# A two-layer diffusion block in split fp32: element-wise sums moved off GpSimd, buffers lent to the gather handed back, one-hots built four at a time, and part of the weights multiplied whole

## The chip, the cores and the metric

The kernel runs on one core of one Trainium2 chip. The metric is the device time of one execution in microseconds (us). TensorE (PE in the profile, PEld for its weight loads) multiplies, VectorE (DVE), ScalarE (ACT) and GpSimd (POOL) do element-wise work, and SyncE (SP) issues most of the transfers.

## The reference, cut to what matters

Two streams of 256 tokens with 1024 features each, `x` and `ctx`, go through two layers. Each layer normalises, multiplies by a wide input matrix, runs three branches (differential attention, windowed attention, a gated delta-net scan), merges them, and then runs an expert layer that keeps 16 of 16,384 experts for each of 8 heads.

```
def token_mixer(h, hc, ...):
    qA, kA, vA, qB, kB, vB, qkvC, zC, aC, bC, gl = split_cols(h @ w_in)
    oA, oB, oC = diff_attention(...), window_gqa(...), gated_deltanet(...)
    return merge_branches((oA, oB, oC), gl, b_gate, w_branch, w_out)

def peer_ffn(h, wq, keys, u_tab, v_tab):
    q = (t @ wq).reshape(n, PEER_HEADS, 2, PEER_HALF)
    s = einsum('thcd,cnd->thcn', q, keys)
    sv, si = top_k(s, 16);  cand = sv[:,:,0,:,None] + sv[:,:,1,None,:]
    cv, ci = top_k(cand, 16)
    eid = (i1 * 128 + i2);  gw = softmax(cv)
    act = gelu(einsum('pd,ped->pe', tb, u_tab[eb]))
    out = einsum('pe,ped->pd', act * gb, v_tab[eb])
```

The second layer needs `ctx` only as keys, values and states; the result is `x`.

## The kernel before, in words

**Arithmetic.** Almost every large product is done in three parts. `split` (line 622 of the kernel before) makes of an fp32 tile of 128x1024 a rounded part on ScalarE (a CAST to fp32r) and a remainder on VectorE (a TENSOR_TENSOR subtract, fp32r out) or, where a caller says so, on GpSimd. `mm3` then multiplies high by high, high by low and low by high. So a loaded half of a weight chunk takes three buffers of 4 KB per partition (the pool `b4`, 36 buffers), one CAST and one subtract before TensorE can use it.

**Stages, in the order of the program.** (1) `ctx` of layer 0: norm, 28 chunks of `w_in` (256 columns each, loaded as two halves), the three branches, merge, output. (2) `route` of `ctx`: queries, top 16 by VectorE's MAX8, FIND_INDEX8 and MATCH_REPLACE8, and the decoding of the indices. (3) The same mixing for `x`. (4) The expert layer of `ctx`, done by gathering: for each of two halves of the tokens 128 indirect DMAs of rows of the first table with a dot product on VectorE (SCALAR_TENSOR_TENSOR with an accumulator), then 128 indirect DMAs of rows of the second table with a product on TensorE. GpSimd issues these DMAs. The rows live in 8 buffers, and three more tiles of the gather too, borrowed from `b4`. (5) The expert layer of `x`, done densely: `route`, then `weights`, which builds for each token a 128x128 table of its expert weights from two one-hot matrices (the stage is called build below) and writes it to HBM, then for all 128 blocks of 128 experts a product with the first table (dU, 8 steps over the features), Gelu, a multiply by the table of weights, and a product with the second table (dV). The first `PRE` blocks of dU may be done ahead of the table. (6) Layer 1: keys, values and states of `ctx`, then mixing, route, build and dense experts for `x`. There is no gather in layer 1.

**What sets the order.** The class `Rec` records all operations, and `order` (line 398) plans on the host, with a cost for every operation, in which order each engine issues them and which buffer each tile takes; the result is emitted as it stands. Operations have priorities by place in the program; `route` and `weights` have a lead of 8000 (`RBASE`). An operation that is far ahead of the oldest unfinished one (measured in `cw`, a sum of planned TensorE, VectorE and ScalarE time) is held back: beyond `FAR` it isn't started, and beyond `NEAR` it has to leave `SPARE` buffers. The gather is a lane of its own. `restore` hands borrowed buffers back: of a borrowed kind whose flag is True, when a tile of that kind is freed after the lane's last operation. Row tiles are freed before the gather's last operation, so their 8 buffers stay lent for the whole of layer 1; the planner's buffers in layer 1's dU are 28 different ones of the 36.

**Who does the subtracts and sums.** `WPOOL` gives GpSimd every second subtract of the weights of `x` in layer 0 (47 of them, with those of `route`). In layer 1, `UP1` gives it 32 of the 64 first blocks of dU, and `VP` seven of eight of the 128 blocks of dV (112). GpSimd also does the sums of rope, of merge and of the output (48 of 128x512), the scaling of matrices in the delta-net chains (144 of 128x256) and in layer 1 the sums and products in `route`.

Every instruction of these helpers is recorded at one line (603 in the profile before), so groups are told apart by tiles and shapes.

## Time and profile before

| | us |
|---|---|
| median of 3 executions | 3939.72 |
| lowest and highest of them | 3938.74, 3962.46 |
| the profiled execution | 3933.92 |
| its span (first to last instruction) | 3932.1 |
| TensorE busy in the span | 3530.0 (90%) |
| VectorE busy | 2472.8 (63%) |
| ScalarE busy | 1610.0 (41%) |
| GpSimd busy | 1481.9 (38%) |
| mean granted TensorE clock | 0.933 of full speed |

The 1.8 us between the profiled execution and its span lie outside the first and last instruction. A matmul's busy time overlaps with that of the next one, so the busy sum of a group divided by its count is what one costs in a row of them, and the mean of one is longer. The granted clock of a stretch is the mean of the two levels (1.2 and 2.4 GHz) that TensorE had in it. A whole fp32 product (not fp32r) shows as two MATMUL records, an fp32r product as one. Where the stages lie in time is known by laying each engine's order of instructions over the records: they agree one by one on VectorE, ScalarE and GpSimd.

### The profile page before, as it was taken

The page shows a single profiled execution, that of the slowest core. Times are in us where ns is not written, and L with a number is a line of the kernel's source. Part 1 is how long each engine was busy: PE and PEld are TensorE (multiplying, and loading weights), DVE is VectorE, ACT ScalarE, POOL GpSimd, SP SyncE. Part 2 cuts the span into 40 slices and gives each one's busy share as a digit, 9 for nine tenths or more (in the row PEclk, how much of TensorE's full clock was granted, in tenths as well). Part 3 has the DMA queues.
Part 4 walks back from the last instruction along what each step waited for, and adds up shares of the span by engine and source line. Part 5 has one row for each costly group of instructions (what it writes and reads, how often), then busy time and mean ns, then how long its engine had stood idle before and what let it go on. Part 6 is the DMA issues. An engine that isn't in the chain of part 4 may idle for free. (4 is left out here: it accounts for less than half of the span.)

```text
span 3932.1 us, 64402 instructions
## 1 busy us (share of the span) xinstructions
PE 3530.0 (90%) x24312; PEld 2982.5 (76%) x24312; DVE 2472.8 (63%) x5599; ACT 1610.0 (41%) x3070; POOL 1481.9 (38%) x1125
## 2 busy tenths in 40 slices
PE   7999964986997798889999999998996899899999
PEld 6787954866794467767777888877896699678998
DVE  4444579889656886897444454646559942555554
ACT  4544422433442233343333346544543343344443
POOL 1110123778364345663333202222023043675443
PEclk9999986877898999999999998988998999999999
DMA  7356742566466799999889851302351455565653
GB/s 279 112 169 239 254 168 98 184 230 233 161 206 231 252 368 376 384 409 361 334 332 333 310 195 43 103 28 89 103 197 65 129 184 170 190 222 213 221 207 142
DMA packets 300966, 837.78 MB, mean 213 GB/s; under 512 B 26736, under 2 KB 96752, under 8 KB 300656
## 3 DMA queue, kind: packets, MB, share of 16 engines
q1 hardware_dynamic: 153168, 522.80, 37.2%
q0 software_dynamic: 73728, 268.47, 18.6%
q10 hardware_dynamic: 73760, 42.40, 3.6%
q8 instruction: 192, 3.15, 0.3%
q14 instruction: 118, 0.97, 0.1%
HBM read 792.67 MB, written 40.89 MB: 212 GB/s over the span
## 5 line engine op out<-in xcount | busy, mean ns | idle before, releaser
L603 PE MATMUL ps<-b,b 128*128 128x256 f32 (+4 forms) x18528 | 2742.4, 309 | 202.7 <-DVE b L603 134.8
L603 PEld LDWEIGHTS ps<-b,b 128*128 128x128 f32 (+2 forms) x18528 | 2449.7, 192 | 476.8 <-DVE b L603 163.3
L603 DVE TENSOR_TENSOR b<-b,b 128x1024 fp32r<-128x1024 f32 (+3 forms) x1065 | 1142.8, 1106 | 817.2 <-ACT b L603 550.9
L603 ACT CAST b<-b 128x1024 fp32r<-128x1024 f32 (+1 forms) x982 | 917.4, 976 | 702.6 <-PE ps L603 297.9
L603 POOL TENSOR_TENSOR b<-b,b 128x1024 fp32r<-128x1024 f32 (+2 forms) x241 | 586.8, 2445 | 922.7 <-DVE b L603 367.5
L603 ACT COPY b<-ps 128x256 f32<-128x256 f32 (+3 forms) x896 | 291.2, 350 | 676.4 <-PE ps L603 666.6
L603 POOL DMA_INDIRECT rows<-in_u_tab,eid x256 | 357.8, 1398 | 271.1 <-DVE rows L603 118.2
L603 POOL DMA_INDIRECT rows<-in_v_tab,eidT x256 | 284.0, 1109 | 426.5 <-PE ps L603 354.6
L603 PE MATMUL ps<-b 128*128 128x128 f32 (+1 forms) x2048 | 337.9, 320 | 19.2 <-ACT b L603 7.5
L603 PE MATMUL ps<-consts,b 128*128 128x128 f32 (+1 forms) x1290 | 261.1, 316 | 103.8 <-DVE b L603 76.9
L603 ACT ACTIVATE b<-ps 128x512 f32<-128x512 f32 (+1 forms) x264 | 136.7, 520 | 523.5 <-PE ps L603 507.0
L603 PEld LDWEIGHTS ps<-b 128*128 128x128 f32 (+1 forms) x2048 | 255.7, 207 | 119.6 <-DVE b L603 39.6
L603 DVE SCALAR_TENSOR_TENSOR rows<-rows,ga 128x1024 f32<-128x1024 f32 x256 | 322.9, 1288 | 4.4 <-DMA rows<-in_u_tab,eid 2.4
L603 PEld LDWEIGHTS ps<-consts,b 128*128 128x128 f32 x1290 | 184.4, 180 | 148.2 <-issue 68.8
L603 DVE TENSOR_SCALAR b<-consts,b 128x128 f32<-128x128 f32 x1024 | 235.4, 309 | 10.8 <-DMA gd<-b 7.7
L603 PE MATMUL ps<-rows,ga 128*32 128x512 f32 x1024 | 160.5, 626 | 19.0 <-DMA rows<-in_v_tab,eidT 17.8
L603 DVE COPY_PREDICATED b<-masks,ps 128x64 f32<-128x64 uint8 (+1 forms) x416 | 83.7, 251 | 148.5 <-PE ps L603 146.9
L603 ACT COPY b<-b 128x128 f32<-128x128 f32 x384 | 108.0, 303 | 60.5 <-DVE b L603 56.1
L603 DVE TENSOR_TENSOR b<-ps,b 128x128 f32<-128x128 f32 (+4 forms) x144 | 61.9, 454 | 93.8 <-PE ps L603 57.8
L603 PEld LDWEIGHTS ps<-rows,ga 128*32 128x32 f32 x1024 | 29.5, 111 | 94.6 <-DMA rows<-in_v_tab,eidT 47.8
L603 PE MATMUL ps<-b,cs 128*32 128x256 f32 x768 | 69.8, 430 | 12.2 <-DVE cs L603 11.5
L603 ACT ACTIVATE b<-b 128x512 f32<-128x512 f32 (+1 forms) x62 | 38.9, 629 | 96.0 <-DVE b L603 42.5
(176 smaller groups left out, 1450.6 us busy)
## 6 DMA issues: line engine op xcount, KB each, us to landing
b<-in_u_cols SPq DMA_DIRECT2D x256, 512.0 KB
b<-in_v_tab SPq DMA_DIRECT2D x256, 512.0 KB
b<-in_w_in SPq DMA_DIRECT2D x184, 512.0 KB
gd<-b ACTq DMA_DIRECT2D x64, 512.0 KB
b<-gd SPq DMA_DIRECT2D x64, 512.0 KB
b<-in_w_ada SPq DMA_DIRECT2D x48, 512.0 KB
b<-in_w_ada SPq DMA_DIRECT2D x96, 256.0 KB
b<-in_wq SPq DMA_DIRECT2D x48, 512.0 KB
```

The costliest lines, as they stand in the source:

```text
L603: r = getattr(getattr(nc, o.eng), o.meth)(*[_real(x) for x in o.args], **{k: _real(x) for k, x in o.kw.items()})
```

## The change

None of the edits changes what is computed:

- GpSimd loses all subtracts (`WPOOL`, `UP1` empty, `VP = 1`), the sums of rope and of the output, and layer 1's work in `route` (`aux` stays VectorE); VectorE takes them. The scalings of the delta-net chains go to ScalarE, one per head. The sums of merge, the square roots, the rope tables and the indirect DMAs stay.
- `restore` hands back every borrowed kind once its lane is done.
- The one-hot of the second index is made for four tokens in one TENSOR_TENSOR of 128x512. Of the four weighted one-hots of the first index, one goes to ScalarE as two activations (`Abs`, then `Relu`), three stay TENSOR_SCALARs on VectorE.
- Layer 0's first 16 chunks of `w_in` for `x` (`WHOLE`) and its first 32 blocks of dU (`U4`) are multiplied in whole fp32: no CAST, no subtract, one product instead of three.
- The planner has new costs, a model of the read port that VectorE and GpSimd share, `PRE` 32 instead of 48, `FAR` 80 instead of 150, no weight in `cw` for `route` and `weights`, and a freer rule for layer 1's first part (`FREE`), once the gather is done.

```diff
-U4, V4 = (), ()
-WPOOL = (1, 3, 5, 7)
-UP0, UP1 = (), range(0, 64, 4)
+U4, V4 = range(32), ()
+WPOOL = ()
+UP0, UP1 = (), ()
-OUTV = False
+OUTV = True
-VP = 8
+VP = 1
+ACTB = (1, 1)
+TAIL, FREE1 = 0, True
+FREE = {"b4": 4, "b2": 2, "b1": 1, "ps": 0}
-PRE = 48
+PRE = 32
-NEAR, FAR = 20.0, 150.0
+NEAR, FAR, URGENT = 20.0, 80.0, 0.0
+WHOLE = range(16)
...
+        o.port = eng in ("vector", "gpsimd") and not o.dma and sum(
+            isinstance(x, V) and x.n > 1 and x.tile.kind == "sb" for x in ins) > 1
...
-        o.cw = self.cw[o.lane] = self.cw.get(o.lane, 0.0) + o.dur * LOAD.get(eng, 0.0)
+        o.lane, o.free = self.lane, self.free
+        o.cw = self.cw[o.lane] = self.cw.get(o.lane, 0.0) + o.dur * LOAD.get(eng, 0.0) * (URGENT if self.base == RBASE else 1.0)
...
-                        if dist > FAR:
+                        free = o.free and lpos[-1] >= len(lanes[-1]) - TAIL
+                        if dist > FAR and not free:
                             return "far"
...
-                if t.tag in BORROW and (not BORROW[t.tag][2] or lpos[lane] == len(lanes[lane])):
-                    restore(t.tag)
+                for tag in BORROW:
+                    if owner.get(tag) == lane and (lpos[lane] == len(lanes[lane]) or tag == t.tag and not BORROW[tag][2]):
+                        restore(tag)
...
         for k in range(n):
-            (lh, ll), (rh, rl) = lhsT(k), rhs(k)
+            a, b = lhsT(k), rhs(k)
+            if len(a) == 1 or len(b) == 1:
+                self.nc.tensor.matmul(out, a[-1], b[-1], start=(start and k == 0), stop=(stop and k == n - 1))
+                continue
+            (lh, ll), (rh, rl) = a[:2], b[:2]
...
-            w = self.g(4, [P, k // 2, n])
-            self.nc.sync.dma_start(w, src[:, h * (k // 2):(h + 1) * (k // 2)])
+            w = self.load([P, k // 2, n], src[:, h * (k // 2):(h + 1) * (k // 2)])
+            if whole:
+                out += [(w[:, j],) for j in range(k // 2)]
+                continue
...
-            nc.gpsimd.tensor_tensor(qv, qv, t1, op=OP.add)
+            nc.vector.tensor_tensor(qv, qv, t1, op=OP.add)
...
-                nc.gpsimd.tensor_tensor(m1, M1[:, None, :].to_broadcast([P, H2, P]), bc(gc), op=OP.mult)
+                for h in range(H2):
+                    nc.scalar.activation(m1[:, h], M1, AF.Copy, scale=gc[:, h:h + 1])
...
+                nc.vector.tensor_tensor(A[:, :, 0], io4, sc[:, 1, k:k + 4, None].to_broadcast([P, 4, P]), op=OP.is_equal)
                 for t in range(4):
                     k = t0 + q + t
-                    nc.vector.tensor_scalar(A[:, t, 0], self.iota, sc[:, 1, k:k + 1], None, OP.is_equal)
-                    nc.vector.tensor_scalar(A[:, t, 1], self.iota, sc[:, 0, k:k + 1], sc[:, 2, k:k + 1],
-                                            OP.is_equal, OP.mult)
+                    if t >= ACTB[l]:
+                        nc.vector.tensor_scalar(A[:, t, 1], self.iota, sc[:, 0, k:k + 1], sc[:, 2, k:k + 1],
+                                                OP.is_equal, OP.mult)
+                    else:
+                        d = A[:, t, 1]
+                        nc.scalar.activation(d, self.iota, AF.Abs, scale=-1.0, bias=sc[:, 0, k:k + 1])
+                        nc.scalar.activation(d, d, AF.Relu, scale=sc[:, 3, k:k + 1], bias=sc[:, 2, k:k + 1])
...
-                if c0 // 2 % 8 in u4:
+                if c0 in u4:
                     for k in range(KT):
-                        nc.tensor.matmul(sp[:, i], u[:, k], full[k // 4][:, k % 4], start=(k == 0), stop=(k == KT - 1))
+                        nc.tensor.matmul(sp[:, i], u[:, k], hT[k][2], start=(k == 0), stop=(k == KT - 1))
                     continue
...
+        self.whole = True
         _, (x, xs) = self.mix(0, 0, self.I["x"], pr, kv, S)
+        self.whole = False
...
-        self.aux = self.nc.gpsimd
+        pass
         self.lab("1 norm1")
+        self.nc.free = FREE1
```

Three places show what the planner makes of it.

TensorE, layer 0, the first chunk of `x` (its result is ps_6821 before, ps_6869 now; the weights are b_1417 and b_1418 before, and b_1409 and b_1410 now; a row with x4 stands for four products), before:

```order
L603 MATMUL ps_6821<-b_1418_6951,b_1470_6732 128x256
L603 MATMUL ps_6821<-b_1417_6780,b_1471_6870 128x256
L603 MATMUL ps_6821<-b_1417_6780,b_1470_6732 128x256
L603 MATMUL ps_6821<-b_1418_6951,b_1470_6732 128x256
L603 MATMUL ps_6821<-b_1417_6780,b_1471_6870 128x256
L603 MATMUL ps_6821<-b_1417_6780,b_1470_6732 128x256
```

and now, with the next chunk (ps_6938) behind it:

```order
L627 MATMUL ps_6869<-b_1409_6822,b_1467_6327 128x256 x4
L627 MATMUL ps_6869<-b_1410_6872,b_1468_6329 128x256 x4
L627 MATMUL ps_6869<-b_1409_6822,b_1467_6327 128x256 x4
L627 MATMUL ps_6869<-b_1410_6872,b_1468_6329 128x256 x4
L627 MATMUL ps_6938<-b_1409_6822,b_1475_6645 128x256 x4
```

The chunk has 48 products before (three for each of two halves of the columns and eight steps) and 16 now, and it has no VectorE subtract ahead of it.

VectorE, layer 1, the start of build (consts holds the ramp 0 to 127, the second operand the indices and weights by token), before:

```order
L603 TENSOR_SCALAR b_5787_30357<-consts_71,b_5777_30336 128x128 x4
L603 TENSOR_SCALAR b_5789_30362<-consts_71,b_5777_30336 128x128 x4
L603 TENSOR_SCALAR b_5791_30367<-consts_71,b_5777_30336 128x128 x2
L603 TENSOR_REDUCE pii_29622<-b_5774_30355 128x2x16 x2
L603 TENSOR_SCALAR b_5791_30367<-consts_71,b_5777_30336 128x128 x2
```

and now:

```order
L627 TENSOR_TENSOR b_5659_29194<-consts_71,b_5649_29190 128x4x128
L627 TENSOR_TENSOR b_5661_29196<-consts_71,b_5649_29190 128x4x128
L627 TENSOR_SCALAR b_5659_29194<-consts_71,b_5649_29190 128x128 x3
L627 TENSOR_SCALAR b_5661_29196<-consts_71,b_5649_29190 128x128 x3
L627 TENSOR_TENSOR b_5663_29198<-consts_71,b_5649_29190 128x4x128
L627 TENSOR_SCALAR b_5663_29198<-consts_71,b_5649_29190 128x128 x3
```

Eight instructions for four tokens have become four on VectorE, and two more stand on ScalarE.

VectorE, layer 1, the dense experts near the middle of dV (128x1024 are subtracts of weights, 128x2x128 the multiply by the table of weights, 128x512 the remainder of its result), before:

```order
L603 TENSOR_TENSOR b_6498_34797<-b_6496_34716,b_6497_34779 128x1024
L603 TENSOR_TENSOR b_6468_34793<-b_6468_34793,b_6469_34628 128x2x128
L603 TENSOR_TENSOR b_6468_34793<-b_6468_34793,b_6470_34646 128x2x128
L603 TENSOR_TENSOR b_6472_34840<-b_6468_34793,b_6471_34831 128x512
L603 TENSOR_TENSOR b_6501_34849<-b_6499_34718,b_6500_34821 128x1024
```

and now:

```order
L627 TENSOR_TENSOR b_6354_33342<-b_6352_33173,b_6353_33329 128x1024
L627 TENSOR_TENSOR b_6357_33354<-b_6355_33180,b_6356_33339 128x1024
L627 TENSOR_TENSOR b_6363_33367<-b_6361_33182,b_6362_33349 128x1024
L627 TENSOR_TENSOR b_6366_33392<-b_6364_33217,b_6365_33380 128x1024
L627 TENSOR_TENSOR b_6340_33421<-b_6340_33421,b_6341_33092 128x2x128
L627 TENSOR_TENSOR b_6340_33421<-b_6340_33421,b_6342_33098 128x2x128
```

The subtracts of dV that stood on GpSimd stand in VectorE's row, ahead of the multiplies; layer 1's last GpSimd work is now the square root of the norm ahead of `route`.

## Rows read from the trace of the kernel before

**Rows 1.** Stretches of the span: length, busy time (count) by engine, granted clock, DMA share, GB/s.

```profile
0.00:495.00 495.00, 464.85 (x3909) 387.58 (x3910) 238.02 (x524) 226.59 (x563) 71.48 (x94) 0.98 0.61 212
495.00:665.00 170.00, 78.86 (x582) 74.93 (x580) 146.49 (x567) 43.61 (x69) 40.51 (x31) 0.71 0.35 120
665.00:1165.00 500.00, 441.52 (x3079) 385.94 (x3078) 381.07 (x702) 210.06 (x489) 333.53 (x255) 0.84 0.60 199
1165.00:1335.00 170.00, 127.10 (x814) 84.55 (x810) 125.30 (x528) 40.22 (x61) 79.78 (x67) 0.87 0.64 229
1335.00:1470.00 135.00, 125.29 (x802) 78.27 (x795) 123.44 (x524) 42.59 (x130) 66.27 (x63) 0.97 1.00 351
1470.00:1830.00 360.00, 318.84 (x1906) 270.65 (x1905) 301.75 (x440) 135.24 (x161) 205.52 (x141) 0.97 1.00 390
1830.00:2330.00 500.00, 496.25 (x3258) 401.99 (x3257) 242.16 (x304) 195.33 (x237) 145.16 (x125) 1.00 0.84 313
2330.00:2870.00 540.00, 504.02 (x3884) 441.63 (x3883) 302.94 (x692) 285.95 (x763) 110.41 (x147) 0.92 0.24 78
2870.00:3055.00 185.00, 133.44 (x1071) 131.26 (x1069) 142.46 (x512) 68.66 (x97) 53.48 (x63) 0.87 0.35 120
3055.00:3170.00 115.00, 110.31 (x522) 77.35 (x522) 115.00 (x503) 41.76 (x130) 3.39 (x1) 0.98 0.51 143
3170.00:3550.00 380.00, 356.33 (x2150) 311.32 (x2149) 161.30 (x136) 155.76 (x184) 212.43 (x84) 0.96 0.56 192
3550.00:3932.00 382.00, 373.23 (x2367) 337.01 (x2365) 192.92 (x175) 164.24 (x192) 159.96 (x57) 0.99 0.54 198
```

**Rows 2.** TensorE's waits, 665 to 1165 us: releaser, us, times, longest.

```profile
PE ps L603 <- DVE b L603: 34.1, 16, 7.8
PE ps L603 <- POOL b L603: 14.9, 5, 7.4
```

**Rows 3.** TensorE's waits, 3170 to 3550 us.

```profile
PE ps L603 <- POOL b L603: 12.3, 9, 2.4
PE ps L603 <- DVE b L603: 6.6, 6, 1.9
PE ps L603 <- ACT b L603: 4.5, 8, 1.0
```

**Rows 4.** TensorE's groups by shape, 3215 to 3290 us: busy us, mean ns, idle before.

```profile
L603 PE MATMUL ps<-b,b 128*128 128x256 f32 x634 | 75.4, 281 | 0.0
```

**Rows 5.** TensorE's groups by shape, whole span.

```profile
L603 PE MATMUL ps<-b,b 64*128 64x512 f32 x64 | 40.7, 719 | 0.7 <-ACT b L603 0.7
L603 PE MATMUL ps<-b,b 64*128 64x256 f32 x192 | 40.1, 415 | 4.6 <-ACT b L603 4.6
```

**Rows 6.** VectorE's groups, 1830 to 2330 us.

```profile
L603 DVE TENSOR_TENSOR b<-b,b 128x1024 fp32r<-128x1024 f32 x148 | 176.8, 1224 | 114.2 <-ACT b L603 67.5 <-PE ps L603 28.5 <-issue 17.7
...
L603 DVE TENSOR_TENSOR b<-b,b 128x512 f32<-128x512 f32 x4 | 2.7, 690 | 0.1
```

**Rows 7.** VectorE's groups, 3600 to 3900 us.

```profile
L603 DVE TENSOR_TENSOR b<-b,b 128x1024 fp32r<-128x1024 f32 x62 | 126.1, 2052 | 62.7 <-ACT b L603 53.0 <-PE ps L603 9.3
```

**Rows 8.** VectorE's groups, 665 to 1165 us.

```profile
L603 DVE SCALAR_TENSOR_TENSOR rows<-rows,ga 128x1024 f32<-128x1024 f32 x115 | 154.9, 1375 | 0.0
L603 DVE TENSOR_TENSOR b<-b,b 128x1024 fp32r<-128x1024 f32 x39 | 66.1, 1698 | 28.5 <-ACT b L603 16.4 <-PE ps L603 10.0 <-POOL b L603 2.0
```

**Rows 9.** GpSimd's groups by shape, whole span.

```profile
L603 POOL TENSOR_TENSOR b<-b,b 128x1024 fp32r<-128x1024 f32 x191 | 505.8, 2658 | 597.0 <-PE ps L603 245.8 <-ACT b L603 227.6 <-DVE b L603 66.7
...
L603 POOL TENSOR_TENSOR b<-b,b 128x512 f32<-128x512 f32 x48 | 79.1, 1649 | 320.8 <-DVE b L603 295.8 <-DVE modT L603 10.3 <-issue 8.7
```

**Rows 10.** VectorE's groups, 3055 to 3170 us.

```profile
L603 DVE TENSOR_SCALAR b<-consts,b 128x128 f32<-128x128 f32 x500 | 112.9, 301 | 0.0
```

**Rows 11.** ScalarE's groups by shape, whole span.

```profile
L603 ACT COPY b<-b 128x128 f32<-128x128 f32 x384 | 108.0, 303 | 60.5 <-DVE b L603 56.1 <-DVE gS L603 2.5 <-ACT b L603 1.1
```

**Rows 12.** Instructions on the gathered rows: ns min/median/max, first and last start.

```profile
L603 PE MATMUL ps<-rows,ga x1024: 592/592/1063, 1159.5 to 2252.9; 128*32 128x512 f32 x171
```

More of the change, by code (lines that the diff above doesn't have):

```diff
@@ L291, in __init__ @@
         self.base = 0
-        self.lane, self.cw = 0, {}
+        self.lane, self.cw, self.free = 0, {}, False
         self.lab = ""
@@ L316, in cost @@
             return max(c * n, 140 if dt == BF else 64) / 2330.0, 0
-        big = max([n] + [x.n for x in ins if isinstance(x, V)])
-        ps = any(isinstance(x, V) and x.tile.kind == "ps" for x in list(ins) + [out])
+        vs = [x for x in ins if isinstance(x, V)]
+        big = max([n] + [x.n for x in vs])
+        ps = any(x.tile.kind == "ps" for x in vs + [out])
+        ptrs = sum(x.n == 1 for x in vs)
         if eng == "scalar":
-            ptr = any(isinstance(kw.get(x), V) for x in ("scale", "bias"))
-            return (0.05 if ps else 0.095) + (0.08 if ptr else 0.0) + big / 1200.0, 0
+            both = all(isinstance(kw.get(x), V) for x in ("scale", "bias"))
+            acc = 0.1 if kw.get("accum_out") is not None else 0.0
+            return (0.05 if ps else 0.095) + (0.19 if both else 0.09 if ptrs else 0.0) + acc + big / 1200.0, 0
@@ L322, in cost @@
         if eng == "vector":
-            two = sum(isinstance(x, V) and x.n > 1 for x in ins) < 2 and not ps and meth in (
-                "tensor_scalar", "tensor_copy", "tensor_single_scalar")
-            if meth == "tensor_tensor" and out.dt == BF and all(x.dt == BF for x in ins if isinstance(x, V)):
+            wide = [x for x in vs if x.n > 1]
+            two = len(wide) < 2 and not ps and not ptrs and meth in ("tensor_scalar", "tensor_copy", "tensor_single_scalar")
+            if meth == "tensor_tensor" and out.dt == BF and all(x.dt == BF for x in vs):
@@ L326, in cost @@
                 two = True
-            ptr = (0.11 if meth == "tensor_scalar" else 0.06) if any(isinstance(x, V) and x.n == 1 for x in ins) else 0.0
-            return (0.125 if ps else 0.065) + ptr + big / (1920.0 if two else 960.0), 0
+            base = 0.065 if not ps or len(wide) > 1 else 0.125
+            if meth in ("max_index", "match_replace") or any(x.dt in (I32, U32) for x in vs):
+                base += 0.06
+            c = base + 0.06 * bool(ptrs) + big / (1920.0 if two else 960.0)
@@ L417, in order @@
             load[tag] = np.cumsum(load[tag])[:N]
-            lent = sum(n for a, n, _ in BORROW.values() if a == tag)
-            assert load[tag].max() <= self.bufs[tag] - lent, (tag, load[tag].max())
+            assert load[tag].max() <= self.bufs[tag], (tag, load[tag].max())
         ready = {e: [] for e in ("tensor", "vector", "scalar", "gpsimd", "sync")}
@@ L460, in borrow @@
             a = BORROW[tag][0]
-            if not slots[a] or load[a][ops_at(owner[a]):].max(initial=0) > cap[a] - 1:
+            if not slots[a] or load[a][ops_at(owner[a]):join.get((owner[tag], owner[a]), N)].max(initial=0) > cap[a] - 1:
                 return False
@@ L633, in split, with load @@
         return hi, lo
+    def load(self, shape, src):
+        t = self.g(4, shape)
+        self.nc.sync.dma_start(t, src)
+        return t
     def ps(self, shape, dt=F32, tag="ps"):
@@ L841, in norm_T @@
         self.to_T(xs, evac)
+        if full:
+            return [(hi[:, j], lo[:, j], f[:, j]) for (hi, lo), f in zip(hT, full) for j in range(4)]
         return [(hi[:, j], lo[:, j]) for hi, lo in hT for j in range(4)]
@@ L845, in norm1 @@
         self.lab(f"{s} norm1")
-        return self.norm_T(self.load_halves(xt), pr["A1"][:, :, s], pr["mod"][:, 0:8, s])
+        full = [self.g(4, [P, 4, T]) for _ in range(2)] if self.whole else None
+        return self.norm_T(self.load_halves(xt), pr["A1"][:, :, s], pr["mod"][:, 0:8, s], full)
     def cut(self, pair, j):
@@ L910, in win @@
             self.lab(lab)
-        return self.load_w(self.I["w_in"][l, CI[name]])
+        return self.load_w(self.I["w_in"][l, CI[name]], self.whole and CI[name] in WHOLE)
     def conv_silu(self, ps, ft0, pr, y):
```

52 lines of the change are left out of this document (34 added, 18 removed).

## The prediction

> **What bounds the kernel now.** First I read the span by stretches that follow the stages [rows 1]: mixing of `ctx` (to 495 us), its route (to 665), mixing of `x` beside the first gathered dots (to 1165), route of `x` (to 1335), build (to 1470), the second gathered dots beside dU and dV (to 1830), the rest of layer 0's dense experts (to 2330), layer 1's mixing (to 2870), route (to 3055), build (to 3170) and dense experts (to the end). The reader is to compare in each row the length with TensorE's busy time and its clock. TensorE is the bound in 1830 to 2330: 496 of 500 us busy at clock 1.00. Over the twelve rows it is idle for 402 us, of which 91 lie in 495 to 665, 58 in 665 to 1165, 43 in 1165 to 1335, 41 in 1470 to 1830, 36 in 2330 to 2870 and 52 in 2870 to 3055; and what it does at a lower clock costs, as busy time by one less the clock, 71 us in 665 to 1165 (0.84) and 40 in 2330 to 2870 (0.92). In the idle stretches VectorE is nearly full: 146 of 170, 123 of 135, 302 of 360, 115 of 115. So layer 0's middle and layer 1's route and build hang on VectorE, the rest on TensorE.
>
> Next, who TensorE waits for: in 665 to 1165 34.1 us for VectorE and 14.9 for GpSimd [rows 2]; in 3170 to 3550 GpSimd comes first [rows 3]. Last, prices by shape. VectorE's subtract of 128x1024 takes 1.224 us in 1830 to 2330, where GpSimd does few sums [rows 6], 1.698 in 665 to 1165 [rows 8] and 2.052 in 3600 to 3900 [rows 7], where GpSimd's own subtracts run beside it at 2.658 [rows 9]. The two slow each other, and what GpSimd takes off VectorE is partly given back.
>
> **The change, part by part,** against the profiled execution of 3933.9 us (span 3932.1 and 1.8 around it; 5.8 under the median).
>
> *Whole fp32.* 16 chunks and 32 blocks, with 16 and 8 products of 256 columns each, make 512 whole products in place of 1536 split ones. The trace has no such product with 128 rows. A split product costs 75.4/634 = 0.119 us in a run without a gap [rows 4], three 0.357. The nearest row has the same width and 64 rows, two records a product: 40.1/96 = 0.418 [rows 5]. The far row above is the 512-wide one, 40.7/32/2 = 0.636 for half its width; below, two records at a split product's price, 0.238. So 512 products cost between -61 and +143 us; I take 0.061 more for each, +31 us, half in `x`'s mixing and half in dU. In return VectorE loses 48 subtracts and GpSimd 16, ScalarE 64 CASTs.
>
> A rule speaks against this: the Trainium skill (FP8 and Floating Point Precision, TensorE Precision Notes) gives true fp32 four passes through the array. By that rule the price would be four against three split products, 512 x 0.119 = +61 us, and the sum below 30 us higher; 0.418 against 0.119 is 3.5 passes, so the trace agrees in direction and is nearer to mine.
>
> *Mixing of `x`, 665 to 1165.* VectorE gets 23 of GpSimd's remaining subtracts (28 us at 1.224) and ten sums of 512 (7 us at 0.690 [rows 6]); it loses 16 chunk subtracts (20 us), and what is left runs undisturbed: 115 dots from 1.375 and 39 subtracts from 1.698 to 1.224 are 36 us [rows 8]. Net -21 of 381. TensorE's 49 us of waits for the two should fall by two thirds, since half of the weights need no subtract: -33. With less idling I put the clock at 0.88, 371 us of work at full speed then taking 422 instead of 442: -20. With +16 for the whole products: -37. Bounds: +16 (nothing filled) and -113 (all idle time and clock lost won back).
>
> *Route of `ctx`, 495 to 665.* The order puts the first chunk at the same place near its end: 0, between -30 and +5.
>
> *Route, build and dense experts of layer 0, 1165 to 2330.* In route TensorE idles 43 us; whole blocks of dU need only their load, and the planner now starts them there, so -40 (0 to -43). Build: 112.9/500 = 0.226 us for a TENSOR_SCALAR [rows 10], 512 are 116 us; now 64 times one sum of 512 (0.690) and three at 0.226, 88 us: -28. The broadcast compare isn't in the trace; between the price of two TENSOR_SCALARs (0.45) and of the four that it replaces (0.90) the term is -44 to -15, and 0.690, that of a sum of its size, lies nearest. ScalarE's added 128 activations at 108.0/384 = 0.281 [rows 11] make 36 us beside its 43 of 135, hidden under VectorE's 88. In 1470 to 1830 half of the 41 idle us go, -20 (0 to -41). +16 for the whole products of dU. Together -72.
>
> *Layer 1's mixing, 2330 to 2870.* Eight more buffers and a longer look-ahead against 36 us idle and 40 of clock: -20 (0 to -76). GpSimd's scalings become two ScalarE activations of 0.28, about 150 of them, 42 us on an engine busy 286 of 540: nothing, unless ScalarE is where a chain waits.
>
> *Layer 1's route, 2870 to 3055.* VectorE takes over 32 subtracts of dU (39 us) and GpSimd's products in route (about 10 of 1.2). It is free for 43 of 185 us, so most fits, but these subtracts queue behind route's own work and TensorE gets its filler later: +15 (0 to +51).
>
> *Layer 1's build.* As above: -28, where VectorE is busy 115 of 115.
>
> *Layer 1's dense experts, 3170 to the end.* 112 subtracts, 137 us, go to VectorE, busy 354 of 762 and less when undisturbed. Queued behind them are the multiplies by the table, and behind these the products. The same form, all subtracts on VectorE, is to be seen in 1830 to 2330 with 4 us idle in 500 at clock 1.00. Here 33 us are idle and 18 lost to the clock; I take -45 (0 to -51).
>
> The first 495 us: 0 (+-15). The sum is -37 -72 -20 +15 -28 -45 = -187: **3747 us**.
>
> **Rivals.** *TensorE fills more.* My terms win back 218 us gross out of 402 idle and about 236 of clock (3530 at 0.933). If buffers, look-ahead and the subtracts' end win back half of the 638, it is -319 + 31: 3646. For it: 91 us idle in 495 to 665, of which I take nothing. Against: route is one chain on VectorE, whatever lies beside.
>
> *The transfers hold the middle.* In 1335 to 1830 the DMA share is 1.00 at 351 to 390 GB/s [rows 1], and the gather's last product starts at 2253 us [rows 12], 80 us ahead of the dense experts' end. The same bytes in less time may not fit. Then the 40 and 20 us of layer 0's route and dU don't come: 3807. Against: VectorE's and TensorE's waits in that stretch are mostly for each other and ScalarE.
>
> *The shorter look-ahead starves TensorE* (slower). `FAR` falls from 150 to 80, in stretches that live on it: 0 to 495 and 2330 to 2870, where busy times clock is 465 x 0.98 + 504 x 0.92 = 919 of 1035 us, 0.89. At 665 to 1165's share (0.742) they take 1239, +204, and with layer 1's -20 lost the time is 3971, within 1%; below that share it is slower. At 0.70, between that row and 1165 to 1335's 0.65, they take 1313: 4045. Against: weights load ahead by buffers too, and in layer 1 `FREE` lifts the limit.
>
> *It does not do what it says.* Its gains come back at the join of the two lanes or at a full buffer pool, and the time stays at 3934. The order shows the subtracts and products moved, so only the gain can fail, not the edit.
>
> **How the numbers follow.** Forecast 0.55, more filled 0.15, transfers 0.18, starved 0.07, nothing 0.05. Faster by over 1% are the first three less a tail of 0.03 near the bound: 0.85; within 1%, about what a measurement of this kernel can tell from no change, 0.08; slower 0.07. The range leaves out the starved case and the outer tails of the others: it goes 26 us below 3646, as whole products may be cheaper, and 83 above 3807, for the 36 more that layer 1's route can cost and for dearer products (47 of the 112 us to their upper bound). That is 3620 to 3890.
>
> **What would show it.** Right: whole products near 0.42 us; VectorE's subtracts near 1.22 everywhere; both builds near 90 us of VectorE; layer 1's dense experts at 99% TensorE and clock 1.00; GpSimd with little but indirect DMAs. Wrong: whole products above 0.6; TensorE's waits for VectorE growing in layer 1's dense experts; DMA share still 1.00 and 1470 to 1830's stage no shorter; the first 495 us longer by over 30.

## The result and the profile after

| | us |
|---|---|
| median of 4 executions after | 3816.06 (3806.39 to 3823.42) |
| median of 4 of the kernel before beside them | 3939.23 (3933.23 to 3962.46) |
| ratio, 95% interval | 0.968, 0.964 to 0.973 |
| the profiled execution, its span | 3817.58, 3815.8 |

The change takes 123 us off, by the two profiled executions 116 (3933.9 to 3817.6), where 187 were forecast. These lines of the page answer to the busy times before; the last is the granted TensorE clock in 40 slices, in tenths.

```profile
span 3815.8 us, 62556 instructions
...
PE 3463.5 (91%) x23800; PEld 2960.3 (78%) x23800; DVE 2374.0 (62%) x5288; ACT 1707.0 (45%) x3554; POOL 818.8 (21%) x716
...
PEclk9996997988899998999999998989997899999999
```

GpSimd's 1482 us have become 819, most of them the issue of indirect DMAs. The stretches of the kernel after follow, cut where VectorE's last instruction of each stage ends; the columns are those of [rows 1].

```profile
0.00:540.20 540.20, 503.61 (x4011) 412.11 (x4012) 252.76 (x549) 258.20 (x652) 47.45 (x56) 0.92 0.56 196
540.20:675.80 135.60, 81.78 (x564) 77.44 (x564) 119.43 (x540) 29.56 (x54) 18.90 (x19) 0.79 0.38 128
675.80:1139.20 463.40, 413.73 (x2727) 353.13 (x2726) 345.58 (x723) 201.65 (x533) 216.89 (x187) 0.89 0.65 227
1139.20:1327.20 188.00, 173.67 (x1172) 134.63 (x1172) 126.15 (x545) 46.79 (x75) 66.83 (x69) 0.97 0.79 285
1327.20:1424.30 97.10, 87.38 (x664) 72.83 (x664) 89.20 (x260) 79.09 (x241) 30.52 (x29) 0.96 0.86 279
1424.30:1834.00 409.70, 363.81 (x1915) 294.33 (x1915) 308.62 (x458) 139.86 (x176) 210.66 (x152) 0.95 0.99 386
1834.00:2263.30 429.30, 418.79 (x2777) 332.06 (x2775) 207.50 (x269) 163.33 (x200) 157.04 (x126) 1.00 0.90 339
2263.30:2843.40 580.10, 542.02 (x4216) 481.89 (x4217) 326.12 (x712) 338.43 (x922) 69.59 (x77) 0.93 0.27 88
2843.40:3001.60 158.20, 99.88 (x806) 98.41 (x804) 129.59 (x539) 55.67 (x83) 0.90 (x2) 0.82 0.26 89
3001.60:3095.80 94.20, 70.45 (x485) 63.31 (x486) 88.45 (x257) 75.67 (x233) 0.00 (x0) 0.92 0.53 151
3095.80:3815.80 720.00, 708.38 (x4480) 640.11 (x4478) 380.62 (x449) 318.73 (x390) 0.00 (x0) 0.99 0.59 202
```

Cut the same way, in both kernels and in the four experiments that the account below rests on, the stages are this long (us of each one's profiled execution; "U" is the stretch of the second gathered dots, "dense" what is left of the dense experts; `before` runs here from 0 to 519 where [rows 1] cut at 495). Executions of one and the same order differ by up to 18 us in a stage: six kernels here with the changed kernel's order in the first stage take 526 to 544 us for it, and `giveback_alone`, which issues what `before` issues until late in layer 0's dense experts, has a mixing of `x` 15 us shorter. The expectations below speak of 402 us for U and of 711 for layer 1's dense experts, as they cut a few us further on.

| | ctx mix | ctx route | x mix | route | build | U | dense | layer 0 | L1 mix | route | build | dense | layer 1 |
|---|---|---|---|---|---|---|---|---|---|---|---|---|---|
| before | 519 | 145 | 499 | 171 | 130 | 363 | 505 | 2332 | 578 | 145 | 113 | 764 | 1600 |
| giveback_alone | 520 | 147 | 484 | 171 | 132 | 358 | 507 | 2319 | 604 | 148 | 127 | 691 | 1570 |
| two_parts | 517 | 142 | 485 | 176 | 130 | 365 | 525 | 2341 | 574 | 139 | 113 | 729 | 1556 |
| split_all | 533 | 132 | 453 | 193 | 140 | 299 | 571 | 2320 | 544 | 158 | 94 | 723 | 1520 |
| after | 540 | 136 | 463 | 188 | 97 | 410 | 429 | 2263 | 580 | 158 | 94 | 720 | 1552 |
| keep_rows | 544 | 136 | 463 | 189 | 97 | 412 | 431 | 2272 | 610 | 173 | 94 | 737 | 1614 |

From before to after, layer 0 is 69 us shorter and layer 1 is 47 shorter. In the first stretch, which was to stay as it was, 21 us are lost.

Next VectorE's groups by shape: two in 676 to 1139 us, one in 3470 to 3816, two in 1327 to 1432.

```profile
L627 DVE SCALAR_TENSOR_TENSOR rows<-rows,ga 128x1024 f32<-128x1024 f32 x123 | 146.9, 1228 | 8.7 <-DMA rows<-in_u_tab,eid 8.7
L627 DVE TENSOR_TENSOR b<-b,b 128x1024 fp32r<-128x1024 f32 x44 | 58.8, 1354 | 26.1 <-ACT b L627 13.2 <-PE ps L627 6.0 <-issue 5.4
...
L627 DVE TENSOR_TENSOR b<-b,b 128x1024 fp32r<-128x1024 f32 x113 | 132.2, 1220 | 32.8 <-issue 32.6 <-ACT b L627 0.2
...
L627 DVE TENSOR_SCALAR b<-consts,b 128x128 f32<-128x128 f32 x192 | 55.6, 350 | 0.0
L627 DVE TENSOR_TENSOR b<-consts,b 128x512 f32<-128x512 f32 x64 | 43.0, 682 | 7.9 <-DMA gd<-b 4.6 <-PE ps L627 2.0 <-ACT b L627 1.3
```

A dot takes 1.228 us instead of 1.375 and a subtract 1.354 instead of 1.698 [rows 8]; in the last dense experts it is 1.220 instead of 2.052 [rows 7]. The last two rows are the one-hots. Their busy times overlap in part (98.6 us together, where VectorE is busy for 89 in that build), so the price is read from starts in a row (start, length, group), here in layer 1's build; the next compare starts at 3041.45.

```profile
3040.08 0.69 DVE L627 TENSOR_TENSOR b<-consts,b 128x512 f32<-128x512 f32 x1
3040.68 0.85 DVE L627 TENSOR_SCALAR b<-consts,b 128x128 f32<-128x128 f32 x3
```

The compare of four tokens takes 0.60 us and three compare-and-multiplies 0.77, or 0.257 each, where the mean of both kinds was 0.226 [rows 10].

The price of a whole product is in TensorE's timeline: 48 records are 24 products with weights that no subtract made.

```profile
1250.91 10.63 PE L627 MATMUL ps<-b,b 128*128 128x256 f32 x48
...
1264.06 7.17 PE L627 MATMUL ps<-b,b 128*128 128x256 f32 x32
```

10.63/24 = 0.443 and 7.17/16 = 0.448 us. Last, VectorE's waits in 1424 to 1834 (what for, us, times, longest):

```profile
DVE rows L627 <- DMA rows<-in_u_tab,eid: 49.5, 14, 37.9
DVE b L627 <- ACT b L627: 31.9, 22, 6.3
DVE b L627 <- DMA b<-gd: 19.5, 1, 19.5
```

Behind layer 0's build VectorE now stands idle, at the head of its queue, for the second gather's first row (38 us; GpSimd issues its transfer only at 1455.5, 31 us after the build's end) and for the table's way back from memory (19.5 us), and the stage grew from 363 to 410 us.

### The profile page after: what moved, and what is told of

Read it like the earlier page. It is cut to its first block, busy times and chain, and to the rows that moved or that the text cites. A ratio compares the mean times of both kernels' runs of the same rounds, so it can differ in the third digit from the quotient of the medians.

```text
span 3815.8 us, 62556 instructions
## 1 busy us (share of the span) xinstructions
PE 3463.5 (91%) x23800; PEld 2960.3 (78%) x23800; DVE 2374.0 (62%) x5288; ACT 1707.0 (45%) x3554; POOL 818.8 (21%) x716
## 4 chain that ended last, share of the span: by engine, by line
PE 49%; DVE 4%; ACT 3%; issue 1%; DMA 1%; ACTq 0%; POOL 0%; POOLq 0%; DVEq 0%
PE ps L627 49%; ACT b L627 3%; DVE b L627 3%; DVE psi L627 0%; DVE psv L627 0%; ACTq L627 0%; DMA gd<-b 0%; DMA b<-in_v_tab 0%; DMA b<-in_u_cols 0%; DVE pii L627 0%; DVE pS L627 0%; DVE pci L627 0%; DVE dst L627 0%; DVE ga L627 0%; POOL qrs L627 0%
## 5 line engine op out<-in xcount | busy, mean ns | idle before, releaser
L627 PEld LDWEIGHTS ps<-b,b 128*128 128x128 f32 (+1 forms) x18016 | 2452.5, 192 | 489.8 <-DVE b L627 141.9
L627 ACT CAST b<-b 128x1024 fp32r<-128x1024 f32 (+1 forms) x918 | 850.2, 972 | 481.3 <-PE ps L627 341.0
L627 DVE SCALAR_TENSOR_TENSOR rows<-rows,ga 128x1024 f32<-128x1024 f32 x256 | 306.1, 1224 | 58.2 <-DMA rows<-in_u_tab,eid 58.2
L627 PE MATMUL ps<-b 128*128 128x128 f32 (+1 forms) x2048 | 272.9, 301 | 37.8 <-ACT b L627 36.7
L627 PEld LDWEIGHTS ps<-b 128*128 128x128 f32 (+1 forms) x2048 | 231.6, 203 | 81.8 <-ACT b L627 60.0
L627 PE MATMUL ps<-rows,ga 128*32 128x512 f32 x1024 | 139.2, 599 | 7.2 <-DMA rows<-in_v_tab,eidT 7.2
L627 POOL TENSOR_TENSOR b<-b,b 128x512 f32<-128x512 f32 x24 | 45.5, 1896 | 351.7 <-DVE b L627 326.2
L627 DVE TENSOR_SCALAR b<-consts,b 128x128 f32<-128x128 f32 x384 | 110.3, 346 | 0.0
L627 DVE TENSOR_TENSOR b<-consts,b 128x512 f32<-128x512 f32 x128 | 87.0, 685 | 13.5 <-DMA gd<-b 8.6
```

Of the source, the lines that this page charges most:

```text
L627: r = getattr(getattr(nc, o.eng), o.meth)(*[_real(x) for x in o.args], **{k: _real(x) for k, x in o.kw.items()})
```

## The experiments

All times are medians; the interval is that of the ratio to runs of the kernel before on the same chip. The changed kernel's own ratio is 0.968 (0.964 to 0.973), so a single piece shows alone only if it is worth about 20 us. Stages are those of one execution each: that of `onehot_old` lies 14 us under its median, those of `split_all`, `half_loads`, `keep_rows` and `gather_first` 14 to 19 above.

**Look-ahead, `far150`.**

```diff
-NEAR, FAR, URGENT = 20.0, 80.0, 0.0
+NEAR, FAR, URGENT = 20.0, 150.0, 0.0
```

> The changed kernel with FAR back at 150. Theory (the short look-ahead leaves the tail of layer 0's ctx attention without filler, and TensorE's clock falls to 0.50 in 300 to 340 us): the front of ctx, which ends at 540 us in the changed kernel and 519 in the one before, ends at 519 to 524, the clock stays at 1.00 there, total 3793 to 3802. Rival (the clock fell there by chance, or for the scalings on ScalarE): it ends at 535 to 545, total 3810 to 3822.

3825.95 us, 0.973 (0.971 to 0.975): above the ranges of theory and rival, and 10 to 17 us slower than the change. The front ends at 524 us instead of 540, as in the theory, but its clock is not 1.00. Here are 300 to 340 us of the kernel before, of the changed kernel, of this run and of `onehot_old` (further on), which has 80 and the changed kernel's order in the front:

```profile
300.00:340.00 40.00, 38.96 (x310) 25.55 (x314) 19.16 (x68) 24.49 (x79) 3.09 (x4) 1.00 0.58 197
300.00:340.00 40.00, 38.32 (x135) 22.88 (x136) 12.79 (x40) 14.36 (x45) 1.23 (x2) 0.50 0.25 95
300.00:340.00 40.00, 37.80 (x180) 24.80 (x180) 15.02 (x48) 17.34 (x55) 3.08 (x4) 0.68 0.20 63
300.00:340.00 40.00, 35.67 (x174) 21.61 (x173) 15.88 (x51) 18.24 (x58) 1.23 (x2) 0.78 0.40 137
```

The changed kernel has 135 records there and a clock of 0.50, that is 1.2 GHz throughout. But with the same order `onehot_old` has 0.78 and a front of 526 us. So the front's length goes with the clock, and that the look-ahead sets this clock is not shown: executions of one order differ by as much. The 16 us are taken back in later stages.

**Bytes of the middle, `half_loads`.** In layer 0, each split block of both tables is loaded by half, and each half is used twice (half of those weights is left out); every engine's order stays the same.

```diff
-                u = self.load([P, KT, P], self.I["u_cols"][l, c0 + i])
+                    u = self.load([P, KT // 2, P], self.I["u_cols"][l, c0 + i][:, 0:KT // 2])
+                    uh, ul = self.split2(u, KT // 2, P)
```

> The changed kernel, with layer 0's split blocks of the first table and all its blocks of the second table loaded by halves (256 instead of 512 KB each); every CAST, subtract and product stays, each half being used twice, and the order of all instructions is the same. Left out: half of these weights. Theory (transfers hold the second gathered dots: 402 us at DMA share 0.99 and 386 GB/s): about 36 MB of some 155 go, and that stage falls from 402 to 310 to 350 us, total 3730 to 3770. Rival (VectorE and the order of the gathered rows hold it): the stage stays at 390 to 402, total 3800 to 3818.

3814.24 us, 0.969 (0.968 to 0.971). The stretch U:

```profile
1426.20:1839.90 413.70, 363.96 (x1916) 294.41 (x1915) 308.87 (x458) 139.73 (x176) 208.51 (x152) 0.95 0.88 315
```

The share falls from 0.99 to 0.88 and the rate from 386 to 315 GB/s, and the stretch takes 414 us, where the change has 410. So the bytes of the split blocks don't hold it. The 32 whole blocks of dU are not halved, though, and they are loaded at the start of U, where VectorE waits 38 us for its first row in both runs. There this run, too, moves 407 GB/s at a share of 1.05:

```profile
1440.00:1480.00 40.00, 20.81 (x83) 6.14 (x81) 10.93 (x17) 2.16 (x4) 24.96 (x26) 0.85 1.05 407
```

Whether transfers make that part long was not tested.

**Whole fp32 undone, `split_all`.**

```diff
-U4, V4 = range(32), ()
+U4, V4 = (), ()
-WHOLE = range(16)
+WHOLE = ()
-        self.whole = True
```

> The changed kernel without whole fp32 (the 16 chunks and 32 blocks split as before). If the whole products pay by sparing VectorE 64 subtracts, as predicted: 3850 to 3890, the loss in layer 0 from 540 to 2263 us. Rival (512 products at 0.06 us more each cost as much as they spare): 3800 to 3825.

3822.58 us, 0.971 (0.969 to 0.973): hardly slower, by the medians, than with whole products, as the rival has it, though layer 0 takes 57 us more (its profiled execution is the slowest of the kernel's four). Route of `x`, the dense experts and layer 1's mixing:

```profile
1118.10:1310.70 192.60, 157.55 (x997) 97.18 (x996) 128.52 (x547) 48.54 (x74) 83.54 (x85) 0.93 0.78 285
...
1749.30:2320.00 570.70, 562.20 (x3695) 462.79 (x3694) 284.43 (x361) 233.25 (x287) 152.17 (x130) 0.99 0.82 303
2320.00:2864.40 544.40, 515.98 (x4133) 460.57 (x4132) 318.72 (x701) 328.15 (x906) 63.98 (x73) 0.95 0.28 93
```

TensorE idles 35 us in route, where it idles 14 with whole blocks, but layer 1's mixing takes 544 us instead of 580. The mixing of `x` is 10 us shorter without whole products (453); what they win lies behind it, and layer 1's mixing gives back more than half of it.

**Subtracts back on GpSimd, `pool_sub`.**

```diff
-WPOOL = ()
-UP0, UP1 = (), ()
-VP = 1
+WPOOL = (1, 3, 5, 7)
+UP0, UP1 = (), range(0, 64, 4)
+VP = 8
```

> The changed kernel with the subtracts back on GpSimd where they were (47 in layer 0's x, 32 in the first blocks of dU and 112 in dV of layer 1). If the two engines' disturbing each other was the cost: layer 1's dense experts go from 711 back to 740 to 765 us, layer 0 loses 10 to 30, total 3860 to 3900. Rival (row buffers and look-ahead made layer 1's gain): dense experts at 705 to 720, total 3805 to 3835.

3841.67 us, 0.977 (0.975 to 0.979), some 26 us slower than the change, between the ranges of theory and rival. Layer 1's dense experts, and VectorE's subtract in 3400 to 3800 us:

```profile
3087.90:3830.20 742.30, 708.40 (x4430) 632.83 (x4429) 413.98 (x310) 317.08 (x389) 371.28 (x138) 0.99 0.56 195
```

```profile
L627 DVE TENSOR_TENSOR b<-b,b 128x1024 fp32r<-128x1024 f32 x71 | 137.0, 1954 | 85.7 <-PE ps L627 36.8 <-ACT b L627 28.1 <-issue 20.4
```

VectorE's 1.220 us is 1.954 here, and the stage 742 us instead of 720, with 34 us of TensorE idle instead of 12. The theory's cause is seen in the stage that it names, at its lower end.

**One-hots as before, `onehot_old`.**

```diff
-ACTB = (1, 1)
+ACTB = (0, 0)
...
-                nc.vector.tensor_tensor(A[:, :, 0], io4, sc[:, 1, k:k + 4, None].to_broadcast([P, 4, P]), op=OP.is_equal)
...
+                    nc.vector.tensor_scalar(A[:, t, 0], self.iota, sc[:, 1, k:k + 1], None, OP.is_equal)
```

> The one-hots are made as before: on VectorE one compare (196 ns apart) and one compare-and-multiply (256 ns apart) a token, none on ScalarE. Theory: VectorE sets the pace of both builds, so layer 0's build goes from 97 us back to about 125, layer 1's from 94 to about 113, and the whole time from 3816 to 3850-3865. Rival: what is lost in the builds is won back in the dense stage behind each, since TensorE has its own backlog there; the builds are as long as in the theory, but the total is 3816-3830.

3807.65 us, 0.969 (0.965 to 0.973): nothing is lost, and the time lies even under the rival's range. Layer 0's build, its dense experts, layer 1's build:

```profile
1306.80:1434.60 127.80, 118.57 (x762) 88.39 (x760) 117.20 (x514) 43.14 (x132) 37.88 (x39) 0.99 0.92 308
...
1838.40:2205.00 366.60, 365.01 (x2437) 292.44 (x2436) 180.85 (x236) 142.23 (x170) 140.95 (x111) 1.00 0.90 334
...
2964.40:3080.60 116.20, 111.75 (x512) 77.26 (x512) 115.93 (x514) 41.35 (x128) 0.00 (x0) 0.98 0.49 139
```

The builds are 31 and 22 us longer, as the theory has it. In layer 0 TensorE gets more done meanwhile (762 records instead of 664 in the build), and its dense experts are 63 us shorter; in layer 1 the dense stage behind gives back 9 us. Layer 1's mixing is 23 us longer (603), and that and the rest of the 22 aren't seen in the medians, whose interval is wider.

**Scalings and small sums back on GpSimd, `pool_rest`.** One of its six edits; the others read the change's diff from plus to minus in the same way.

```diff
-            nc.vector.tensor_tensor(qv, qv, t1, op=OP.add)
+            nc.gpsimd.tensor_tensor(qv, qv, t1, op=OP.add)
```

> The small sums and the delta scalings go back to GpSimd (scalings of 128x256 at 0.65-0.72 us each, rotary sums, the sums behind the second layer's dense stage); the 128x1024 subtracts stay on VectorE. Theory: only the wide subtracts cost anything, as they alone met VectorE's own for long; 3816 plus or minus 10. Rival: a scaling on GpSimd stands in the chain of the recurrence, and the sums lengthen VectorE's two-operand work beside them; both mixings of the layers get longer by 10-20 us each, 3836-3856.

3809.10 us, 0.969 (0.966 to 0.973). The theory holds: they are worth nothing that shows. Layer 1's route is 146 us again, as before the change, instead of 158, and its dense experts are 731 instead of 720.

**Slots kept, `keep_rows`.**

```diff
-                for tag in BORROW:
-                    if owner.get(tag) == lane and (lpos[lane] == len(lanes[lane]) or tag == t.tag and not BORROW[tag][2]):
-                        restore(tag)
+                if t.tag in BORROW and (not BORROW[t.tag][2] or lpos[lane] == len(lanes[lane])):
+                    restore(t.tag)
```

> The eight row slots (4 KB each) stay lent to the end, as before. Theory: given back they feed the second layer's look-ahead, and half of the 45 us that layer 1's dense stage gained is theirs (the other half went with the wide subtracts); layer 1 from its mixing on gets longer by 20-40 us, 3836-3856. Rival: TensorE is busy 99% of layer 1's dense stage and 36 slots less 8 are enough there; 3816 plus or minus 8.

3871.27 us, 0.986 (0.982 to 0.990): 55 us slower, above the theory's 20 to 40. Every engine issues the same until layer 0's dense experts are nearly done. Layer 1's mixing is 30 us longer, its route 14, its dense experts 17. (Its profiled execution is 17 us above its median.) In the mixing, this is the delta-net recurrence, first with the slots kept, then the changed kernel's:

```profile
2350.00:2390.00 40.00, 40.00 (x212) 31.36 (x212) 11.05 (x45) 22.53 (x95) 0.00 (x0) 0.50 0.10 29
2390.00:2430.00 40.00, 39.65 (x218) 31.39 (x217) 13.63 (x45) 23.70 (x85) 0.00 (x0) 0.56 0.00 1
```

```profile
2340.00:2380.00 40.00, 39.56 (x286) 32.26 (x284) 18.29 (x58) 29.46 (x108) 1.07 (x1) 0.78 0.16 52
2380.00:2420.00 40.00, 39.42 (x343) 35.09 (x343) 20.78 (x52) 30.11 (x93) 7.48 (x6) 1.00 0.30 96
```

With the slots kept next to nothing is loaded there (29 and 1 GB/s), TensorE has the chain's small products, and its clock is at the lower level for most of the 80 us: 430 records where the changed kernel has 629.

**Gather ranked higher, `gather_first`.**

```diff
-GBASE, RBASE = 0, -8000
+GBASE, RBASE = -1000, -8000
```

> The gathered expert rows get a higher rank than the build and the dense blocks beside them, so that the second gather's rows are asked for earlier; nothing else is changed. Theory: the stage after layer 0's build is 402 us long because VectorE stands at its queue's head for the second gather's first rows (38 us) and for the table's way back from memory (19 us) while TensorE runs dry behind it; with the rows earlier that stage gets shorter by 20-50 us, 3766-3796. Rival: the wait only moves (the first half of the rows or the build waits instead) and the sum of route, build and that stage stays at about 695 us; 3816 plus or minus 10.

3810.52 us, 0.970 (0.967 to 0.974). VectorE's waits in the stretch U fall as the theory foresaw:

```profile
DVE rows L627 <- DMA rows<-in_u_tab,eid: 21.9, 21, 2.5
DVE b L627 <- DMA b<-gd: 7.6, 1, 7.6
```

69.0 us of waits have become 29.5, and the stretch 358 us instead of 410. But route is 206 instead of 188 and the dense experts 464 instead of 429: route, build, U and dense come to 1125 us, where the change has 1124. The rival is right in total; the wait for the first row was not what set the stages' sum.

**Parts of the change alone, in the kernel before.** `giveback_alone` has the new call of `restore` (the diff of `keep_rows` read from plus to minus) and the change's new bound in the check before a buffer is lent, which `keep_rows` doesn't take back; `nopool_alone` has the new `WPOOL`, `UP1` and `VP` (that of `pool_sub`, likewise), `two_parts` both.

> The kernel before, with one thing of the change: the row slots come back when the gathered experts have ended. Theory (the slots are the largest part, whatever GpSimd does): undoing it cost 55-68 us, so alone it brings layer 1's mixing, route and dense experts 40-65 us; 3870-3895 where before has about 3936. Rival (the slots help only with the subtracts on VectorE, because slower GpSimd subtracts hold the buffers, or because the larger look-ahead of before uses them elsewhere): 3915-3940.

3890.83 us, 0.986 (0.984 to 0.988): 55 us faster, the theory's total, but not in its places: layer 1's mixing is 26 us longer, its route and build 17, and only its dense experts are shorter, by 74. Layer 1's route, build and dense experts:

```profile
2923.00:3071.10 148.10, 121.37 (x938) 119.06 (x937) 126.44 (x488) 58.49 (x82) 55.99 (x63) 0.89 0.26 91
3071.10:3197.70 126.60, 118.84 (x740) 98.25 (x739) 126.60 (x513) 52.80 (x143) 12.83 (x6) 0.96 0.60 179
3197.70:3888.60 690.90, 667.16 (x4093) 592.63 (x4092) 327.58 (x304) 292.39 (x349) 339.55 (x130) 0.99 0.56 200
```

TensorE does 938 records in route and 740 in build, 732 and 512 before: dense work has moved into stretches in which VectorE's chain left it idle. In the changed kernel that doesn't happen: route and build have 806 and 485 records with the slots given back, 805 and 490 with them kept. So the 55 us alone and the 55 undone lie in different stages.

> The kernel before, with one thing of the change: all 128x1024 subtracts of weights, columns and table blocks on VectorE. Theory (the two engines' subtracts slow each other, and TensorE waits for GpSimd's): 25-35 us less than before, 3900-3912, most of it in layer 1's dense experts. Rival (VectorE is the bound in layer 0's middle and in layer 1's route, so the added subtracts come back there): 3930-3950.

3931.03 us, 0.997 (0.995 to 0.999): 12 to 15 us, about half of what the theory says and within the rival's range. Layer 1's dense experts gain 18 (746 us), the dense experts of layer 0 lose 19 (524 instead of 505).

> The kernel before with both: slots given back and all these subtracts on VectorE; one-hots, whole products, scalings, small sums, look-ahead and the planner's costs as before. Theory (these two carry the change and add up): 80-100 us less than before, 3836-3856, within 20-40 us of the changed kernel. Rival (each works only with the planner's new costs and settings): no more than the better of the two alone, 3870-3910.

3899.37 us, 0.989 (0.987 to 0.992): 43 to 47 us, no more than the slots alone, the rival's result. In layer 1 the two do add up to something (1556 us, with 1570 and 1580 alone and 1600 before). Layer 0 is as long as before: its routes of `ctx` and of `x` still leave TensorE idle for 80 and 49 us, after the whole change 54 and 14.

```profile
516.60:658.70 142.10, 62.39 (x467) 60.42 (x467) 125.92 (x547) 34.48 (x55) 29.77 (x24) 0.72 0.31 104
...
1144.00:1320.30 176.30, 127.05 (x843) 87.02 (x841) 122.13 (x536) 40.10 (x60) 62.07 (x60) 0.84 0.62 222
```

**The long look-ahead in the front only, `far_first`.**

```diff
-                        if dist > FAR and not free:
+                        if dist > (150.0 if now < 500.0 else FAR) and not free:
```

> The changed kernel with the longer look-ahead of before (150) for the first 500 us of the planner's own count and the new one (80) behind it. Theory: the front gets the 16 us back that it got with 150 throughout, and the rest stays as it is: 3795-3805 where the changed kernel has about 3816. Rival: what the front gains is taken back where the stages join, as with 150 throughout; 3811-3826.

3813.97 us, 0.967 (0.964 to 0.969), not to be told from the change, as the rival has it. The first three stages:

```profile
0.00:522.40 522.40, 486.96 (x4013) 403.97 (x4014) 255.87 (x547) 254.34 (x649) 48.82 (x58) 0.96 0.60 209
522.40:666.30 143.90, 65.55 (x474) 62.40 (x473) 124.23 (x547) 29.04 (x47) 28.44 (x24) 0.72 0.34 113
666.30:1155.30 489.00, 444.15 (x2917) 367.74 (x2918) 342.44 (x725) 207.01 (x544) 231.69 (x204) 0.89 0.68 236
```

The front gains 18 us, with as many records (4013, in the change 4011). TensorE then does 474 records in the route of `ctx` instead of 564 and idles 78 us there instead of 54, and `x`'s mixing has 2917 left to do instead of 2727: at its end the run is 16 us behind. No run beat the changed kernel by more than the intervals.

## Why the prediction was right in sign and too large

The forecast's side, and its range, hold; of the 187 us 71 are missing from the profiled 116. Over the span TensorE's idle time fell from 402 to 352 us, and what its lower clock costs (busy time by one less the clock) from 236 to 215: some 70 us, where the terms, the two builds left out, were to win back some 160. The rest of the gain is busy time, most plainly in the builds: in layer 1's, 512 records counted as 109 us busy at VectorE's pace, and 485 count as 70 now.

One reading was off. VectorE was called nearly full where TensorE idles, but of the rows named 123 of 135 and 115 of 115 us are the builds, where TensorE was idle for 10 and 5 us only; in the route of `x` and in layer 1's, which idle 43 and 52, VectorE was busy for 125 of 170 and 142 of 185. (The 33 us idle in layer 1's dense experts are 32.) By the forecast's steps:

*Whole fp32*, +31: 0.443 and 0.448 us against three split products' 0.357 make 44 to 47. The row with 64 rows that it was taken from (0.418) was a little low. The Trainium skill (FP8 and Floating Point Precision, TensorE Precision Notes) gives true fp32 four passes, by [rows 4] an estimate of 0.476 us; the measured price lies between the two.

*The first 495 us*, 0: +21, outside the 15 allowed. The clock is the reason as far as the rows show it: in 300 to 340 us it is 0.50 with 135 records. The forecast priced a clock lost there only as a rival for the whole kernel and not in the sum; but other executions of the same order lose as little as 6 us. *Route of `ctx`*, 0: -10: VectorE, whose chain it is, is busy for 119 us there instead of 131, and TensorE does 564 records instead of 477.

*Mixing of `x`*, -37: -36, but not by its terms. The waits for VectorE and GpSimd were to fall by 33 of 49 us, and fell by 11. TensorE's wait for VectorE in 676 to 1139 us:

```profile
PE ps L627 <- DVE b L627: 38.0, 15, 9.7
```

The other 25 or so are the clock, 0.89 where 0.84 was, as forecast in kind. With all products split the stage is shorter still (453), and with `before`'s own order `giveback_alone` has 484 instead of 499. So the number was partly luck. *Layer 1's route*, +15: +14, by another cause: with the subtracts alone moved to VectorE (`nopool_alone`, `two_parts`) the stage is 141 and 139 us long, not longer than the 145 of before, and with route's own sums and products back on GpSimd (`pool_rest`) it is 146, while with the subtracts alone back there (`pool_sub`) it is 160. So route's own work makes it longer, and not the queued subtracts. *Layer 1's dense experts*, -45: -44, right for half of its reason: with the subtracts back on GpSimd the stage is 22 us longer, and with the slots kept 17. The forecast gave it all to the subtracts.

*Route, build and dense experts of layer 0*, -72: -44, the step that failed most. Its parts stand in the trace: TensorE's idle time in route fell from 43 to 14 us, and VectorE's time in the build from 119 to 89. But route itself became 17 us longer, and the -20 in U didn't come: its idle time is 46 where it was 42. The first line is VectorE's wait for TensorE in route, 6.9 us before; the second is TensorE's wait in U for loads of dU's blocks, of which there was none before:

```profile
DVE b L627 <- PE ps L627: 23.3, 11, 5.3
...
PE ps L627 <- DMA b<-in_u_cols: 19.0, 2, 14.7
```

So the dense products that fill route seem to delay its chain, and whole blocks need no subtract but still wait for their load. The mistake was to add up idle time stage by stage, as if each us filled were a us gained. The account that fits the runs is that TensorE's dense work is one stock that the stages draw on: work pulled into one stretch is missing in the next. `onehot_old`, `gather_first`, `far_first` and `split_all` each move 20 to 60 us between stages and the total by less than can be measured.

*Layer 1's mixing*, -20: +2. The slots have no fixed worth there: undone, they cost 30 us; given back alone they lengthen the stage by 26. What its length does go with is the dense stage ahead of it: in the changed kernel and the eight experiments on it that give the slots back it falls from 603 us behind 367 (`onehot_old`) to 544 behind 571 (`split_all`), with 560 to 585 between. That fits the stock, as a longer dense stage leaves time for work of layer 1 beside it, but no run shows it by itself. *Layer 1's build*, -28: -19. VectorE's time is 88 us as forecast (by two errors that cancel: the compare is cheaper than 0.690, the multiplies are dearer than 0.226), the stage 94, and the new wait is for ScalarE, which is busy for 76 of them and late most often. TensorE's waits there, 3001 to 3096 us:

```profile
PE ps L627 <- ACT b L627: 23.0, 34, 1.3
```

Of the forecast's signs of being wrong one came: in U the DMA share is still 0.99, and the stage is no shorter. That is the sign of *The transfers hold the middle*, which has the nearest number (3807). For the stretch as a whole its cause falls with `half_loads`, 18% less traffic and the same length; for the first 90 us of U, where rows, loads and table are waited for, it stays open. *The shorter look-ahead starves TensorE* is seen at most in 300 to 340 us, and with 150 the total is longer. *It does not do what it says* had a part of what happened: gains of one stage came back in the next.

Where the 123 us come from, by the ladder of ratios: before 1, `two_parts` 0.989 (slots and subtracts, nearly all in layer 1, 43 us), `split_all` 0.971 (all but whole products, 70 us more), after 0.968 (whole products, 11 us, within the intervals). Undone alone, the slots cost 55 to 69 us, the subtracts 26 to 34, the look-ahead 10 to 17, the others 11 or less. The 70 us of the middle step are not put down to one edit: one-hots and small sums together with scalings cost nothing when undone, and the planner's new costs, `PRE`, `URGENT` and `FREE` were not tried alone. That stays open.

## What to carry to other kernels

When one engine is 90% busy with work that can be done early, read its idle time and its lost clock over the whole span, not by stage: filling a gap there gains only what isn't then missing further on, or taken from the chain whose gap it was. Look first for buffers that stay reserved after their use, since a look-ahead without buffers both idles TensorE (27 us more in layer 1's route and dense experts with the slots kept) and lowers its clock (0.87 instead of 0.93 in layer 1's mixing). Before the pieces of a change are added up, undo the largest one alone, and add it alone too: here the two differ.

## What the runs showed of the hardware that was not expected

TensorE's clock falls to its lower level while the engine counts as busy: 40.00 of 40.00 us busy and a granted clock of 0.50 (1.2 GHz) in 2350 to 2390 with the slots kept, in a stretch of small products, 212 records, that follow one another at the chain's pace. Busy time doesn't tell it, and neither does a lack of loads: in 2750 to 2790 of the same run TensorE counts 40.00 us busy too, with 272 records, 1 GB/s and a clock of 1.00. So the granted clock has to be read beside the busy time.

The compare of 128x512 with an operand spread along 128 columns takes 0.682 us by its mean, a sum of its size 0.690 [rows 6], so the spreading costs nothing that shows.

VectorE's subtract beside GpSimd's own (2.716 us each in `pool_sub`) takes 1.954 us instead of 1.220 in the mean, but the mean hides two cases: of the 71, 43 take 1.21 to 1.23 us, 19 take 3.2 to 3.5, and 9 lie between. Here is one that starts inside GpSimd's:

```profile
3762.51 2.40 POOL L627 TENSOR_TENSOR b<-b,b 128x1024 fp32r<-128x1024 f32 x1 [8.85 <-issue]
3763.74 2.26 DVE L627 TENSOR_TENSOR b<-b,b 128x1024 fp32r<-128x1024 f32 x1 [5.58 <-PE ps L627]
```

GpSimd's ends at 3764.91 and VectorE's at 3766.00, 1.09 us later, so nearly all of VectorE's work comes after GpSimd's instruction. It does not run slowly beside it, it waits it out.
